# Evacuating projections from PSUM: both heads on ScalarE first, then both on VectorE, in a hybrid attention layer

## The chip, the cores and the metric

The kernel runs on one core of one Trainium2 chip. The metric is the device time of one execution in microseconds; the time before is the median of three runs, 699.13 us (698.71 to 699.32).

## The reference, cut to what matters

One encoder layer with 1024 positions of width 1024 in fp32. The input is normalised and modulated to `u`. One projection gives queries, keys, values and gates for 8 heads of forgetting attention (FoX) and 8 of stick-breaking attention, head width 64, and 8 forget-gate columns.

```python
h = u @ w_in[layer]
fq, fk, fv, fg, ff, sq, sk, sv, sg = _split_columns(h)
log_f = jax.nn.log_sigmoid(ff + b_f[layer])
f_cum = jnp.cumsum(log_f, axis=1).transpose(0, 2, 1)
...
# FoX, per block of 128 queries
s = einsum('bhqd,bhkd->bhqk', q, k) * scale + (f_q[..., :, None] - f_k[..., None, :])
p = softmax(where(causal, s, -inf));  out = p @ v
# stick-breaking
log_beta, log_keep = log_sigmoid(z), where(strict, log_sigmoid(-z), 0)
w = where(strict, exp(log_beta + cumsum_from_the_right(log_keep) - log_keep), 0);  out = w @ v
...
y = concatenate([y_fox * silu(fg), y_sb * silu(sg)]) @ w_out[layer]
x = layer_norm(alpha * x + gate * y)
```

## The kernel before, in words

**Tiling.** Heads go in eight pairs p, the two heads h of a pair on the lower and the upper 64 partitions. Pairs 0 to 3 are stick-breaking, 4 to 7 FoX. Queries go in eight blocks i of 128 positions. To keep fp32 precision every operand of TensorE is split into a high part, rounded to the matmul's format, and a low part, the remainder, and each product is made of three matmuls (hi x hi, hi x lo, lo x hi).

**Projections.** `gen_m(p, m)` makes the queries (m = 0), keys (1) or gates (2) of a pair in two chunks `ch` of 512 positions: 24 matmuls (L256 to L258) into one PSUM accumulator `m` of 64 + 64 partitions, then its evacuation. `evac_q` (L227) writes for each head the high part with ScalarE (L232) and the low part with VectorE (L233), `evac_k` (L236) likewise (L241, L244) and sends the high part to the other half of the partitions by a DMA on SyncE's queue (L243). `v_tile` (L305) makes 128 positions of the values of two pairs (L311 to L313) and evacuates them in two halves, one for each pair, with ScalarE (L319) and VectorE (L320); for one group it also takes the forget-gate columns (L323). There are two accumulators of this kind (`acc`), and TensorE can start a third chunk only when the first has been read in full.

**Attention.** `att_query` copies a query block to a padded tile `qz` (ScalarE, L389). `att_scores` makes the scores S (L411, L412) in a single PSUM buffer. In stick-breaking, ScalarE makes `kp` and `be` with two sigmoids (L430, L431), VectorE scans `kp` (L436, L440), and GpSimd multiplies it into `be` (L442, after a memset at L443). In FoX, VectorE adds the forget bias `fb` and takes the row's extreme (L418), adds the causal mask to the next block's part of `fb` (L396), ScalarE does the exponential (L423), VectorE a reciprocal (L424) and GpSimd the scaling (L425). `att_transpose` transposes the weights to a PSUM tile T (L459, two buffers) and splits it into `pt`: the high part by ScalarE (L461), the low part by VectorE (L462). `att_pv` multiplies them with the values (L474): first the products with the high part of `pt`, then those with the low part. Its sum is evacuated by ScalarE, VectorE and GpSimd in turn (L493 to L495).

**The forget logs** (`forget_logs`, L339) need Exp and Ln on ScalarE (L344, L345) between operations on VectorE (L343, L346, L349). Sigmoid, Exp and Ln lie in different function tables, and each change of table shows as an ACT_TABLE_LOAD.

**Weights** come in by DMA (`raw`) and are split by GpSimd into `whi` and `wlo` (L125, L126). GpSimd and VectorE also prepare the output gate early on (L698 to L701).

**What sets the order.** TensorE's order is written by hand: attention units and steps of the projections ("fillers") are interleaved by a table. During the start SyncE's is as well. The order of VectorE, ScalarE, GpSimd and the DMA queues in the main part is set by a scheduler that goes by a model of the engines' times; each engine then runs its instructions in that order. Where a wait by TensorE is short, those orders have placed the evacuations between attention operations.

Of the kernel before, what the change touches and what calls it, by code (L numbers as in the profile page):

```python
# [8 lines left out]
F32 = mybir.dt.float32  # L9
F32R = mybir.dt.float32r  # L10
AF = mybir.ActivationFunctionType
ALU = mybir.AluOpType

P = 128
# [4 lines left out]
HD = 64  # L19
EPS = 1e-5  # L20
ALPHA = 2.0 ** 0.25
SCALE = HD ** -0.5
# [5 lines left out]
def tile_hybrid_layer(  # L28
# [17 lines left out]
    nc = tc.nc  # L46
# [180 lines left out]
    def evac_q(p, ch, acc, qst, heads):  # L227
        s = slice(ch * 512, ch * 512 + 512)
        for h in heads:
            r = slice(h * HD, h * HD + HD)  # L230
            o = slice((1 - h) * HD, (1 - h) * HD + HD)
            nc.scalar.activation(qst[h][r, s], acc[r, :], AF.Copy, scale=SCALE)  # L232
            nc.vector.scalar_tensor_tensor(qst[h][o, s], acc[r, :], SCALE, qst[h].bitcast(F32)[r, s],  # L233
                                           op0=ALU.mult, op1=ALU.subtract)

    def evac_k(p, ch, acc, kst, klo, heads):  # L236
        s = slice(ch * 512, ch * 512 + 512)
        for h in heads:
            r = slice(h * HD, h * HD + HD)
            o = slice((1 - h) * HD, (1 - h) * HD + HD)  # L240
            first = nc.scalar.copy(kst[h][r, s], acc[r, :])  # L241
            kf = kst[h].bitcast(F32)
            nc.sync.dma_start(kf[o, s], kf[r, s])  # L243
            last = nc.vector.tensor_tensor(klo[r, s], acc[r, :], kf[r, s], op=ALU.subtract)  # L244
        return first, last

# [13 lines left out]
    qst, kst, klo, sgt, vt = {}, {}, {}, {}, {}  # L260
# [11 lines left out]
    def evac_m(p, m, ch, acc, heads=(0, 1)):  # L272
        if m == 0:
            evac_q(p, ch, acc, qst[p], heads)
        elif m == 1:
            return evac_k(p, ch, acc, kst[p], klo[p], heads)
        else:
            evac_g(p, ch, acc, sgt[p])
# [26 lines left out]
    def v_tile(g, t, acc, quarters):  # L305
        n = 264 if g == 1 else 256
        ts_ = slice(t * P, (t + 1) * P)
        for kt in range(NB):
            hi, lo = quarters[kt // 2]
            s = slice((kt % 2) * n, (kt % 2) * n + n)  # L310
            nc.tensor.matmul(acc[:, :n], u_hi[kt][:, ts_], hi[:, s], start=(kt == 0), stop=False)  # L311
            nc.tensor.matmul(acc[:, :n], u_lo[kt][:, ts_], hi[:, s], start=False, stop=False)  # L312
            nc.tensor.matmul(acc[:, :n], u_hi[kt][:, ts_], lo[:, s], start=False, stop=(kt == NB - 1))  # L313
            if kt == 3:
                yield
        for i in range(2):
            v4 = vt[2 * g + i].rearrange("p t (x c) -> p t x c", c=HD)
            a4 = acc[:, i * P:(i + 1) * P].rearrange("p (x c) -> p x c", c=HD)
            nc.scalar.copy(v4[:, t, 0::2, :], a4)  # L319
            nc.vector.tensor_tensor(v4[:, t, 1::2, :], a4, v4.bitcast(F32)[:, t, 0::2, :],  # L320
                                    op=ALU.subtract)
        if g == 1:
            nc.vector.tensor_tensor(fsb[:, :, t], acc[:, 256:264], bf_sb, op=ALU.add)  # L323
        yield

    def gen_v(g, quarters=None, tiles=range(NB)):
        n = 264 if g == 1 else 256
        if quarters is None:
            quarters = []
            for h in range(4):  # L330
                src = w_vf[h] if g == 1 else w_v[g - (g > 1), h]
                quarters.append(fetch_w(f"v{g}_{h}", src, 2 * n))
        yield
        if g:
            make_v(g)
        for t in tiles:
            yield from v_tile(g, t, acc_tile(f"v_{g}_{t}"), quarters)
# [387 lines left out]
    def v_first(t, acc):  # L725
        for _ in v_tile(0, t, acc, v0_w):
            pass
# [9 lines left out]
    for kb in range(NB):  # L737
# [5 lines left out]
        if kb < len(evacs):  # L743
            n, h = evacs[kb]
# [204 lines left out]
    for k in range(len(units) + LAG + 1):  # L949
        if k < len(units):  # L950
# [10 lines left out]
            p, h, i = units[k]  # L961
# [85 lines left out]
```

## Time and profile before

| | |
|---|---|
| median of three runs | 699.13 us |
| profiled execution | 699.99 us |
| its span, first to last instruction | 698.2 us |
| granted TensorE clock, mean | 0.996 |
| TensorE (PE) busy | 676.0 us, 4033 matmuls |
| VectorE (DVE) busy | 483.7 us |
| GpSimd (POOL) busy | 410.6 us |
| ScalarE (ACT) busy | 385.0 us |
| evacuation of a query chunk, per head | 0.59 us ScalarE (L232), 0.69 us VectorE (L233) |
| of a value tile, per pair | 0.27 us ScalarE (L319), 0.28 us VectorE (L320) |

The profile is of one execution; a row of the timeline has the start in us from the span's start, the duration in us, the engine, the line, the operation with its output and input, their shapes, the count, and in brackets how long the engine had been idle and what released it. A row of the waits has the waiting engine and line, the one waited for, the total in us, how many times, and the longest. A row grouped by line has its busy time and the mean of one in ns, then the idle time ahead of it with its releasers.

### The profile page before, as it was taken

To read this page: it belongs to the slowest core of one execution; us is meant where nothing else is said; L and a number is where in the kernel's file an instruction comes from. 1 tells how busy PE (TensorE), PEld (TensorE's weight loads), DVE (VectorE), ACT (ScalarE), POOL (GpSimd) and SP (SyncE) were. 2 spreads that over 40 slices of the span, in tenths; PEclk is the share of its full clock that TensorE was granted. 3 is DMA by queue.
4 is the path that set the end of the run, shared out by engine and by line. 5 is a ranking of instruction groups with operands and counts; after the bars stand their busy time and mean duration, and the time that the engine had idled before them with its cause. 6 is when DMAs were issued, how large, how long until landed. Compare 5 with 4: busy or idle time off the path is not lost.

```text
span 698.2 us, 11781 instructions
## 1 busy us (share of the span) xinstructions
PE 676.0 (97%) x4033; PEld 589.0 (84%) x4033; DVE 483.7 (69%) x931; ACT 385.0 (55%) x866; POOL 410.6 (59%) x530
## 2 busy tenths in 40 slices
PE   7999989999999999999999999999999999999995
PEld 4789887888997888889988877889988889888884
DVE  5985678767657676767686684758576767784644
ACT  5667567856658576666664554645564666531000
POOL 4560487656437566556388897868483464665412
PEclk9999999999999999999999999999999999999998
DMA  8953451112102122112144554345241299143301
GB/s 313 415 215 128 113 176 53 28 39 49 42 9 69 40 53 55 38 46 61 29 134 145 174 164 155 112 116 164 95 143 51 58 283 364 56 162 113 119 31 60
DMA packets 44027, 81.59 MB, mean 117 GB/s; under 512 B 5120, under 2 KB 18880, under 8 KB 43072
## 3 DMA queue, kind: packets, MB, share of 16 engines
q1 hardware_dynamic: 42816, 76.65, 33.5%
q10 hardware_dynamic: 1152, 4.19, 2.0%
q8 instruction: 32, 0.52, 0.3%
q14 instruction: 27, 0.22, 0.1%
HBM read 60.34 MB, written 16.29 MB: 110 GB/s over the span
## 4 chain that ended last, share of the span: by engine, by line
PE 76%; DVE 7%; DMA 5%; POOL 4%; ACT 4%; issue 3%; SPq 0%; POOLq 0%; DVEq 0%; ACTq 0%
PE pv L474 9%; PE m L256 8%; PE m L257 8%; PE m L258 8%; PE T L459 8%; PE o L835 4%; PE o L833 4%; PE o L834 4%; PE S L412 4%; PE S L411 4%; PE v L311 3%; PE v L313 3%; PE v L312 3%; DMA wss<-in_w_ss_dram 1%; DMA raw<-in_w_qkg_dram 1%
## 5 line engine op out<-in xcount | busy, mean ns | idle before, releaser
L256 PE MATMUL m<-uh,whi 128*128 128x512 f32 x304 | 126.3, 415 | 0.5 <-DVE kl L244 0.5
L257 PE MATMUL m<-ul,whi 128*128 128x512 f32 x304 | 119.8, 394 | 0.0
L258 PE MATMUL m<-uh,wlo 128*128 128x512 f32 x304 | 119.6, 394 | 0.0
L462 DVE TENSOR_TENSOR pt<-T,pt 128x512 fp32r<-128x512 f32 (+2 forms) x192 | 100.6, 550 | 16.1 <-ACT pt L461 14.9
L442 POOL TENSOR_TENSOR be<-be,kp 128x127 f32<-128x127 f32 (+3 forms) x64 | 77.1, 1205 | 34.9 <-DVE kp L440 25.9
L461 ACT CAST pt<-T 128x512 fp32r<-128x512 f32 (+2 forms) x192 | 85.7, 480 | 17.2 <-PE T L459 13.6
L436 DVE TENSOR_TENSOR_SCAN kp<-kp,floor 128x512 f32<-128x512 f32 (+2 forms) x64 | 65.2, 1018 | 32.4 <-ACT kp L430 31.4
L474 PE MATMUL pv<-pt,v 128*128 128x256 f32 (+3 forms) x640 | 81.7, 272 | 3.8 <-DVE pt L462 3.8
L474 PEld LDWEIGHTS pv<-pt,v 128*128 128x128 f32 (+1 forms) x640 | 77.4, 163 | 9.0 <-DVE pt L462 4.7
L425 POOL TENSOR_SCALAR a<-a,l 128x1024 f32<-128x1024 f32 (+3 forms) x64 | 48.3, 755 | 43.8 <-DVE l L424 31.2
L423 ACT ACTIVATE a<-a,nm 128x1024 f32<-128x1024 f32 (+3 forms) x64 | 49.8, 778 | 40.5 <-DVE nm L418 40.1
L258 PEld LDWEIGHTS m<-uh,wlo 128*128 128x128 f32 x304 | 57.1, 188 | 13.5
L411 PE MATMUL S<-k,q 128*128 128x512 f32 (+5 forms) x192 | 66.6, 348 | 1.5 <-ACT be L431 0.8
L412 PE MATMUL S<-kl,qz 128*128 128x512 f32 (+5 forms) x192 | 65.5, 342 | 0.0
L256 PEld LDWEIGHTS m<-uh,whi 128*128 128x128 f32 x304 | 57.3, 188 | 9.2 <-DVE kl L244 0.9
L257 PEld LDWEIGHTS m<-ul,whi 128*128 128x128 f32 x304 | 57.4, 189 | 8.0
L495 POOL TENSOR_TENSOR ty<-ty,sg 64x256 f32<-64x256 f32 x64 | 47.7, 745 | 26.5 <-DVE ty L494 12.5
L418 DVE CUSTOM_DVE_ANT_0 a<-S,fb 128x1024 f32<-128x1024 f32 (+3 forms) x64 | 48.2, 754 | 15.9 <-PE S L412 7.8
L430 ACT ACTIVATE kp<-S 128x128 f32<-128x128 f32 (+3 forms) x64 | 41.7, 651 | 31.9 <-PE S L412 28.6
L311 PE MATMUL v<-whi_v,uh 128*128 128x256 f32 (+1 forms) x192 | 56.0, 292 | 0.7 <-DVE kl L244 0.7
L389 ACT CAST qz<-q 64x128 fp32r<-64x128 f32 x128 | 37.4, 295 | 31.3 <-PE S L412 30.0
L313 PE MATMUL v<-wlo_v,uh 128*128 128x256 f32 (+1 forms) x192 | 54.2, 282 | 0.0
(284 smaller groups left out, 1628.6 us busy)
## 6 DMA issues: line engine op xcount, KB each, us to landing
raw<-in_w_qkg_dram SPq DMA_DIRECT2D x38, 256.0 KB, 3.0
wss<-in_w_ss_dram SPq DMA_DIRECT2D x7, 1024.0 KB, 9.0
x<-in_x_dram SPq DMA_DIRECT2D x8, 512.0 KB, 7.1
k<-k SPq DMA_DIRECT2D x32, 128.0 KB, 2.3
wg<-in_w_gate_dram SPq DMA_DIRECT2D x8, 512.0 KB, 5.0
raw_o<-in_w_out_dram SPq DMA_DIRECT2D x16, 256.0 KB, 2.7
fb<-f_dr ACTq DMA_DIRECT2D x8, 512.0 KB, 4.3
wo_dr<-whi_o SPq DMA_DIRECT2D x16, 256.0 KB, 2.4
```

The costliest lines, as they stand in the source:

```text
L256: nc.tensor.matmul(acc, hi[:, c], u_hi[kt][:, s], start=(kt == 0), stop=False)
L257: nc.tensor.matmul(acc, hi[:, c], u_lo[kt][:, s], start=False, stop=False)
L258: nc.tensor.matmul(acc, lo[:, c], u_hi[kt][:, s], start=False, stop=(kt == NB - 1))
L311: nc.tensor.matmul(acc[:, :n], u_hi[kt][:, ts_], hi[:, s], start=(kt == 0), stop=False)
L313: nc.tensor.matmul(acc[:, :n], u_hi[kt][:, ts_], lo[:, s], start=False, stop=(kt == NB - 1))
L411: nc.tensor.matmul(S[:, s, :w], qst[p][h][:, qs], kst[p][h][:, ks], start=True, stop=False)
L412: nc.tensor.matmul(S[:, s, :w], z, klo[p][:, ks], start=False, stop=True)
L436: nc.vector.tensor_tensor_scan(rv, rv, floor[0][:, 512 - n:][:, ::-1], initial=0.0, op0=ALU.mult, op1=ALU.max)
L442: nc.gpsimd.tensor_tensor(be[:, :ke - 1], be[:, :ke - 1], kp[:, 1:ke], op=ALU.mult)
L461: nc.scalar.copy(hi[:, :n, qo:qo + P], t3)
L462: nc.vector.tensor_tensor(lo[:, :n, qo:qo + P], t3, hi.bitcast(F32)[:, :n, qo:qo + P], op=ALU.subtract)
L474: nc.tensor.matmul(acc[:m, q0:256], vt[p][:, kb, h * P:h * P + m], pt[:, kb % 4, q0:], start=start, stop=stop)
```

## The change

Per accumulator there are two heads, or two pairs for values. Before, ScalarE and VectorE took turns: high part of head 0, low part of head 0, high part of head 1, low part of head 1. After, ScalarE writes both high parts, then VectorE both low parts. The same operations on the same data, in `evac_q`, `evac_k` and `v_tile`:

```diff
     def evac_q(p, ch, acc, qst, heads):
         for h in heads:
             r = slice(h * HD, h * HD + HD)
+            nc.scalar.activation(qst[h][r, s], acc[r, :], AF.Copy, scale=SCALE)
+        for h in heads:
+            r = slice(h * HD, h * HD + HD)
             o = slice((1 - h) * HD, (1 - h) * HD + HD)
-            nc.scalar.activation(qst[h][r, s], acc[r, :], AF.Copy, scale=SCALE)
             nc.vector.scalar_tensor_tensor(qst[h][o, s], acc[r, :], SCALE, qst[h].bitcast(F32)[r, s],
                                            op0=ALU.mult, op1=ALU.subtract)
...
     def evac_k(p, ch, acc, kst, klo, heads):
             first = nc.scalar.copy(kst[h][r, s], acc[r, :])
             kf = kst[h].bitcast(F32)
             nc.sync.dma_start(kf[o, s], kf[r, s])
+        for h in heads:
+            r = slice(h * HD, h * HD + HD)
+            kf = kst[h].bitcast(F32)
             last = nc.vector.tensor_tensor(klo[r, s], acc[r, :], kf[r, s], op=ALU.subtract)
...
     def v_tile(g, t, acc, quarters):
-        for i in range(2):
-            v4 = vt[2 * g + i].rearrange("p t (x c) -> p t x c", c=HD)
-            a4 = acc[:, i * P:(i + 1) * P].rearrange("p (x c) -> p x c", c=HD)
+        v4s = [vt[2 * g + i].rearrange("p t (x c) -> p t x c", c=HD) for i in range(2)]
+        a4s = [acc[:, i * P:(i + 1) * P].rearrange("p (x c) -> p x c", c=HD) for i in range(2)]
+        for v4, a4 in zip(v4s, a4s):
             nc.scalar.copy(v4[:, t, 0::2, :], a4)
+        for v4, a4 in zip(v4s, a4s):
             nc.vector.tensor_tensor(v4[:, t, 1::2, :], a4, v4.bitcast(F32)[:, t, 0::2, :],
                                     op=ALU.subtract)
```

The four reads of one accumulator stay in sequence. Before, each of them waits for the one ahead of it on the other engine. After, ScalarE's second follows its first without a wait, VectorE's first waits for both of ScalarE's, and VectorE's second waits for nothing more. TensorE's order is the same row by row; the scheduler's order on the other engines changes around the evacuations, and ScalarE has 812 instructions in place of 811.

VectorE at the evacuation of q_5, chunk 1 (near 394 us), before and then after. `q_0` and `q_1` are the two heads' halves, `m_0_1` the accumulator, `pt` the low part of transposed weights of pair 4, `a`, `nm` the FoX scores' evacuation (`S_1_7`: head 1, block 7), which is two rows:

```order
L233 SCALAR_TENSOR_TENSOR q_0_4446<-m_0_1_4559,q_0_4446 64x512
L462 TENSOR_TENSOR pt_4_0_1_0_4585<-T_0_2_0_4638,pt_4_0_1_0_4584 128x3x128
L418 ISA a_1_7_4661,nm_1_7_4662<-S_1_7_4656,fb_4121 128x1024
L418 ISA nm_1_7_4662 128x1
L233 SCALAR_TENSOR_TENSOR q_1_4447<-m_0_1_4559,q_1_4447 64x512
```

The same place on VectorE after the change:

```order
L235 SCALAR_TENSOR_TENSOR q_0_4446<-m_0_1_4559,q_0_4446 64x512
L235 SCALAR_TENSOR_TENSOR q_1_4447<-m_0_1_4559,q_1_4447 64x512
L424 ISA a_1_7_4661,nm_1_7_4662<-S_1_7_4656,fb_4121 128x1024
L424 ISA nm_1_7_4662 128x1
L468 TENSOR_TENSOR pt_4_0_1_0_4585<-T_0_2_0_4638,pt_4_0_1_0_4584 128x3x128
```

The second half moved up to the first, and `pt` moved behind the second half and behind the scores.

VectorE at the evacuation of k_6, chunk 1 (near 468 us), before and then after; `fb` is the causal mask's addition, `kl` the low part of the keys:

```order
L396 TENSOR_TENSOR fb_5482<-fb_5482,causal 128x128
L244 TENSOR_TENSOR kl_5316<-m_1_1_5421,k_0_5314 64x512
L462 TENSOR_TENSOR pt_5_0_1_0_5456<-T_0_2_0_5502,pt_5_0_1_0_5455 128x3x128
L418 ISA a_1_7_5537,nm_1_7_5538<-S_1_7_5532,fb_5047 128x1024
L418 ISA nm_1_7_5538 128x1
L244 TENSOR_TENSOR kl_5316<-m_1_1_5421,k_1_5315 64x512
```

The same place on VectorE after the change:

```order
L402 TENSOR_TENSOR fb_5482<-fb_5482,causal 128x128
L249 TENSOR_TENSOR kl_5316<-m_1_1_5421,k_0_5314 64x512
L249 TENSOR_TENSOR kl_5316<-m_1_1_5421,k_1_5315 64x512
L424 ISA a_1_7_5537,nm_1_7_5538<-S_1_7_5532,fb_5047 128x1024
L424 ISA nm_1_7_5538 128x1
L468 TENSOR_TENSOR pt_5_0_1_0_5456<-T_0_2_0_5502,pt_5_0_1_0_5455 128x3x128
```

Again `pt` went from the place behind the first half to the place behind the second half and the scores. In q_4 and k_4, chunk 1, `pt` moved behind the second half alone. In k_5 and q_6, chunk 1, the scores' L418 stands first, then the two halves, then `fb`, then the two rows of `pt`, which had stood ahead of `fb` and of the second half. In q_7, chunk 1, L418 and the two halves stand ahead of `pt`; in k_7, chunk 1, the two halves stand together ahead of the scores of the last block.

ScalarE around the forget logs (212 to 220 us), before and then after. `fab` is the log's working tile, `kp`, `be` the sigmoids of the stick-breaking pair 1 (head 1, block 7) and of the next pair:

```order
L430 ACTIVATE kp_1_7_2471<-S_1_7_2466 128x1024
L431 ACTIVATE be_1_7_2472<-S_1_7_2466 128x1024
L389 CAST qz_83<-q_1_1564 64x128
L344 ACT_TABLE_LOAD
L344 ACTIVATE fab<-fab 128x64
L345 ACT_TABLE_LOAD
L345 ACTIVATE fab<-fab 128x64
L461 CAST pt_1_1_2_0_2433<-T_1_5_0_2494 128x4x128
L461 CAST pt_1_1_2_1_2442<-T_1_5_1_2501 128x2x128
L430 ACT_TABLE_LOAD
```

The same place on ScalarE after the change:

```order
L350 ACT_TABLE_LOAD
L350 ACTIVATE fab<-fab 128x64
L436 ACT_TABLE_LOAD
L436 ACTIVATE kp_1_7_2471<-S_1_7_2466 128x1024
L437 ACTIVATE be_1_7_2472<-S_1_7_2466 128x1024
L395 CAST qz_83<-q_1_1564 64x128
L351 ACT_TABLE_LOAD
L351 ACTIVATE fab<-fab 128x64
L467 CAST pt_1_1_2_0_2433<-T_1_5_0_2494 128x4x128
L467 CAST pt_1_1_2_1_2442<-T_1_5_1_2501 128x2x128
L436 ACT_TABLE_LOAD
```

Exp moved ahead of `kp` and `be`, and one more table load stands between them.

## The prediction

> **What bounds the kernel now.** I read the head of the profile's page and its chain first.
>
> ```profile
> span 698.2 us, 11781 instructions
> PE 676.0 (97%) x4033; PEld 589.0 (84%) x4033; DVE 483.7 (69%) x931; ACT 385.0 (55%) x866; POOL 410.6 (59%) x530
> PE 76%; DVE 7%; DMA 5%; POOL 4%; ACT 4%; issue 3%; SPq 0%; POOLq 0%; DVEq 0%; ACTq 0%
> ```
>
> TensorE is busy for 97% of the span and carries 76% of the chain. VectorE, at 69%, and ScalarE, at 55%, matter only where TensorE has to wait for them, so the next view is the list of what TensorE waits for (in all, times, longest).
>
> ```profile
> PE pv L474 <- DVE pt L462: 3.8, 5, 1.6
> ...
> PE T L459 <- POOL be L443: 1.1, 1, 1.1
> ...
> PE S L411 <- ACT be L431: 0.8, 1, 0.8
> ...
> PE m L256 <- DVE kl L244: 0.5, 1, 0.5
> ```
>
> The largest wait, 3.8 us, is for pt, the low half of the transposed weights (L462), not for an evacuation. Evacuations reach TensorE directly for 0.5 us at L256. So there is little to win, and the question is what the new order does to the work that shares an in-order engine with the evacuations. The rows grouped by line give prices (busy in all, mean ns of one, then idle before).
>
> ```profile
> L320 DVE TENSOR_TENSOR v<-v,v 128x128 fp32r<-128x128 f32 x60 | 17.0, 284 | 9.3 <-ACT v L319 8.7
> L233 DVE SCALAR_TENSOR_TENSOR q<-m,q 64x512 fp32r<-64x512 f32 x24 | 16.5, 689 | 5.7 <-ACT q L232 5.1
> ```
>
> **What the change does to a pair.** No evacuation is added or removed; each pair stays two ScalarE operations (0.59 us) and two VectorE operations (0.69 us for both kinds), one after the other (the 0.59 stands in the rows of q_5 below), 2.56 us for a query or key chunk. Three hand-overs between engines become one. A hand-over costs almost nothing: in the group of rows around 395 us below, ScalarE's half ends at 393.62 and VectorE's starts at 393.65. Two fewer hand-overs are worth 0.06 us. What counts is that VectorE now starts one ScalarE operation later (some 0.5 to 0.59 us), then runs 1.38 us in one piece, and that whatever stood between the halves stands elsewhere. A value pair is small (0.28 us an operation on VectorE), and TensorE's waits name no value evacuation, so I count the value tiles at nothing: the matmuls of the next tile cover them; bare, each would cost or win up to 0.28 us.
>
> **q_5, chunk 1, near 394 us: +1.5 us.** Rows of ScalarE, VectorE and TensorE:
>
> ```profile
> 393.03 0.59 ACT L232 ACTIVATE q<-m 64x512 fp32r<-64x512 f32 x1 [1.55 <-PE m L258]
> 393.65 0.68 DVE L233 SCALAR_TENSOR_TENSOR q<-m,q 64x512 fp32r<-64x512 f32 x1 [0.27 <-ACT q L232]
> 394.37 0.56 DVE L462 TENSOR_TENSOR pt<-T,pt 128x384 fp32r<-128x384 f32 x1
> 394.84 1.22 DVE L418 CUSTOM_DVE_ANT_0 a<-S,fb 128x1024 f32<-128x1024 f32 x1
> 395.49 1.00 PE L474 MATMUL pv<-pt,v 128*128 128x256 f32 x8
> ```
>
> Today pt is done at 394.93. Afterwards both ScalarE halves end at about 394.2 (393.03 + 2 x 0.59), then 0.68 and 0.69 for the VectorE halves (395.55), 1.22 for L418 (396.8), 0.56 for pt: 397.35. TensorE's eight products start at 395.49 on the high half of pt; at 0.12 us each the three of them last until 395.85, where the low half is needed. 397.35 - 395.85 = 1.5 us of waiting. Bounds: 1.0, if L418 can't start ahead and pt slips in faster than its row, and 2.0, if a hold-up like that of L396 (below) falls in.
>
> **k_6, chunk 1, near 468 us: +1.9 us.** VectorE and TensorE:
>
> ```profile
> 467.80 0.67 DVE L244 TENSOR_TENSOR kl<-m,k 64x512 fp32r<-64x512 f32 x1
> 468.40 0.54 DVE L462 TENSOR_TENSOR pt<-T,pt 128x384 fp32r<-128x384 f32 x1
> 468.87 1.20 DVE L418 CUSTOM_DVE_ANT_0 a<-S,fb 128x1024 f32<-128x1024 f32 x1
> 469.00 0.74 PE L474 MATMUL pv<-pt,v 128*64 128x256 f32 x5 [0.15 <-DVE pt L462]
> ```
>
> Here TensorE already waits 0.15 us for pt, so there is no slack. The first half starts when it does today, since both of ScalarE's operations are done before; then pt moves behind the second half (0.69) and L418 (1.20): 1.89 us later, all of it on the path. Bounds 1.2 (only L418) and 2.4.
>
> **Four like places: +2.6 us.** In q_4 chunk 1 (304 us), k_4 chunk 1 (320), k_5 chunk 1 (414) and q_6 chunk 1 (450) pt also goes behind the second half. The first of them:
>
> ```profile
> 303.57 0.42 DVE L462 TENSOR_TENSOR pt<-T,pt 128x256 fp32r<-128x256 f32 x1
> 304.22 0.58 PE L474 MATMUL pv<-pt,v 128*128 128x256 f32 x4
> ```
>
> pt starts 0.69 us later for the second half and up to 0.5 more because the first now waits for ScalarE's second operation: 303.57 + 1.2 + 0.42 = 305.2. Two of the four products use the high half, so the low one is needed at 304.5: 0.7 us. Each place lies between 0 (pt hidden) and 1.2 (both delays bare); I take 0.65 for each of the four. In the other chunks that the change reorders, pt has over 2 us until its product, or is not moved: nothing.
>
> **The forget logs, 212 to 221 us: +2.5 us.** ScalarE, VectorE, GpSimd, TensorE:
>
> ```profile
> 212.26 1.03 ACT L430 ACTIVATE kp<-S 128x1024 f32<-128x1024 f32 x1
> ...
> 214.54 1.28 ACT L344 ACT_TABLE_LOAD   x1
> 215.83 0.26 ACT L344 ACTIVATE fab<-fab 128x64 f32<-128x64 f32 x1
> ```
>
> ```profile
> 213.44 0.87 DVE L343 SCALAR_TENSOR_TENSOR fab<-fsb 128x64 f32<-128x64 f32 x1
> 214.23 1.21 DVE L436 TENSOR_TENSOR_SCAN kp<-kp,floor 128x512 f32<-128x512 f32 x1
> 215.48 1.28 DVE L440 TENSOR_TENSOR_SCAN kp<-kp,floor 128x512 f32<-128x512 f32 x1
> 217.69 1.23 DVE L346 SCALAR_TENSOR_TENSOR flf<-fsb,fab 128x64 f32<-128x64 f32 x1 [0.94 <-ACT fab L345]
> 218.95 1.26 DVE L349 TENSOR_TENSOR_SCAN fsb<-flf,later 128x64 f32<-128x64 f32 x1
> ```
>
> ```profile
> 216.84 2.00 POOL L442 TENSOR_TENSOR be<-be,kp 128x1023 f32<-128x1023 f32 x1 [0.47 <-DVE kp L440]
> 218.79 2.51 POOL L126 TENSOR_TENSOR wlo<-raw,whi 128x512 fp32r<-128x512 f32 x2
> ```
>
> ```profile
> 220.85 0.98 PE L474 MATMUL pv<-pt,v 128*64 128x256 f32 x7 [1.64 <-DVE pt L462]
> ```
>
> Because the value tile before it is evacuated differently, the scheduler puts Exp (L344) ahead of the last kp and be of the second head, and so needs one more table load on ScalarE. Exp cannot start before L343 ends at 214.31. From there: 0.26 for Exp, 1.28 for the load, two sigmoids of 1.03 (217.9; qz after them fits in their overlap), the load for Ln 1.28, Ln 0.26: 219.5, where L346 starts at 217.69 today. Kp is ready at 216.9, its two scans (1.21 and 1.28) end at 219.4, and GpSimd's 2.00 us product runs to about 221.4. That matters: L346 and L349 have 64 elements a lane, yet took 1.23 and 1.26 us, and ended within 0.1 us of a GpSimd operation's end (218.84; the first of the two at 218.79, about 220.05). Held in the same way, L346 ends at 221.45, L349 near 222.7, and TensorE resumes 0.64 us after its end, as today (220.85 against 220.21): 223.35. Without the hold-up, at 0.28 us each (the L320 row), VectorE would be free at about 220.1, as today, and TensorE lose some 0.4 us to ScalarE's later high part. So +0.4 to +2.9; I take 2.5, since both rows are held today. The Trainium skill, "SBUF — State Buffer", section "Who interferes with whom", has a VectorE instruction with two SBUF inputs blocked for the whole of a GpSimd instruction that reads SBUF; this trace agrees (1.23 us for 64 elements), and by that rule the upper part of the span is the right one.
>
> On the load itself the rows say 1.28 us, with Exp 0.01 us behind it. The Trainium skill, "ScalarE: Activation LUTs", section "What ACT_TABLE_LOAD costs", adds a drain of about 1.38 us to each switch; by it the sum would be 1.4 us higher, and this trace does not show it.
>
> **What is won: -0.7 us at 90 to 99 us, and -0.5 at 562.**
>
> ```profile
> 90.59 0.59 ACT L232 ACTIVATE q<-st_q1b 64x512 fp32r<-64x512 f32 x1 [1.40 <-DVE q L233]
> ...
> 94.67 0.58 ACT L241 CAST k<-st_k1b 64x512 fp32r<-64x512 f32 x1 [1.32 <-DVE kl L244]
> ```
>
> ```profile
> 92.06 1.31 POOL L699 TENSOR_TENSOR gate<-gate,wg 128x512 f32<-128x512 f32 x1 [1.06 <-ACT wg L698]
> ```
>
> ScalarE's second key half waited 1.32 us for VectorE, and be, behind it on ScalarE, held TensorE for 0.8 us (the S row of TensorE's waits). That wait goes. Next late is GpSimd's be, for which TensorE's first transpose waits 1.1 us; it moves forward only as far as GpSimd's gate sums do, whose 1.06 us of waiting for ScalarE shrinks too, as ScalarE no longer waits 1.40 us at 90.59. Between 0 (GpSimd unmoved) and -0.8 (all of it); I take -0.7. At 562 the second half of k_7 stood behind L418 and held an accumulator: the 0.5 us of the L256 row of TensorE's waits goes.
>
> **Sum.** 1.5 + 1.9 + 2.6 + 2.5 - 0.7 - 0.5 = +7.3 us on the profiled execution's 699.99 (span 698.2 and 1.8 around it), 707.3. That execution lies 0.86 above the median of 699.13, so I forecast 706.4.
>
> **Rivals.** *Faster.* Accumulators come free as a pair, TensorE's next chunk starts earlier, and pt is fast enough everywhere: it holds if TensorE's products have more queued ahead of the low half than I count. For it speak TensorE's waits that the halves in turn cause now: 0.8 for be, 0.5 at L256 and about half of the 1.1 for GpSimd's be, -1.9 us in all: 697.2. It decides at 468 us: there the low half is needed the moment it is ready, which speaks against it. Chance 0.09. *No change*: only 468 us hurts (+1.9), and the two gains (-1.2) nearly pay for it: 699.8; chance 0.08. *Half of it*: GpSimd does not hold L346, and the four like places are half hidden: 1.5 + 1.9 + 0.6 + 0.3 - 1.2 = +3.1, 702.2; chance 0.20. *Worse*: at k_5 and q_6, L396 now stands ahead of pt, and one such operation was held for a long time:
>
> ```profile
> 404.77 4.15 DVE L396 TENSOR_TENSOR fb<-fb,causal 128x128 f32<-128x128 f32 x1
> ```
>
> If one or both meet a busy GpSimd, pt comes some 1.3 us later at each (one L126, 2.51 for two): about +3, 709.4; chance 0.13. The forecast keeps 0.50.
>
> **Chances and range.** The measurement can tell about 0.2%, 1.4 us. Faster 0.09, same 0.08, slower 0.83, which are the cases above. The range reaches from below the half case, 701.0, to the worse case, 709.8; the first two rivals, 0.17, lie outside.
>
> **What would show it.** Right: TensorE's waits for pt grow from 3.8 us to about 10, with single waits near 1.5 to 2 us at q_5 and k_6 chunk 1; one more table load, and L346 over 1 us long; no wait for be near 95 us. Wrong: products at q_5 and k_6 that start without a wait for pt, or a forget stretch that is not longer than today's 8.6 us (212.26 to 220.85).

## The result, and the profile after

The changed kernel takes 708.24 us, median of 4 runs (708.14 to 709.12), against 699.12 (698.71 to 699.32): 1.0133 times as long, interval 1.012 to 1.0147, or 9.1 us more. The forecast was 706.4, the range 701.0 to 709.8.

The profiled execution took 708.33. The head of its page, then the list of what TensorE waits for (in all, times, longest):

```profile
span 706.6 us, 11831 instructions
PE 680.3 (96%) x4033; PEld 592.7 (84%) x4033; DVE 481.7 (68%) x931; ACT 386.4 (55%) x867; POOL 411.0 (58%) x530
```

```profile
PE pv L480 <- DVE pt L468: 11.0, 9, 2.6
...
PE S L417 <- ACT be L437: 0.8, 2, 0.5
PE pv L480 <- ACT pt L467: 0.5, 1, 0.5
```

The wait for pt grew from 3.8 to 11.0 us. TensorE's busy time grew too, from 676.0 to 680.3 us, with the same 4033 matmuls, so part of the loss is no wait: the matmuls themselves took longer somewhere. The rows in which the evacuations held TensorE (v and m, both waiting for kl) are gone.

TensorE's order is the same in both kernels, so each matmul's start can be set against its start before. Where that difference jumps, time went or came. Up to 540 us:

| place (time before) | jump, us | running total |
|---|---|---|
| 96 us, first be | -0.94 | -0.8 |
| 99 us, GpSimd's be | -1.24 | -2.2 |
| 180 us, k_2 | -0.90 | -3.1 |
| 215 to 221 us, forget logs: four waits | +0.33, +0.66, +0.65, +0.96 | -0.35 |
| 221 to 224 us: no wait, slower matmuls | +1.6 | +1.25 |
| 269 us, k_3 | +0.5 | +1.8 |
| q_4, k_4 | +0.96, +0.74 | +3.6 |
| q_5 | +1.66 | +5.2 |
| 410 us; k_5 | -0.85; +0.85 | +5.1 |
| 434 us, the mask's L396 | -1.28 | +3.8 |
| q_6 | +1.64 | +5.4 |
| k_6 | +1.98 | +7.4 |
| 469 to 472 us: no wait, slower matmuls | +1.55 | +9.0 |

At q_7 -0.66 and +0.62 cancel, k_7 gives -0.53, and it ends at +8.4, the difference of the spans. The -0.85 and the -1.28 are not the change's: a kernel below that keeps the turns from 200 us on (early_only) shows the same jumps there, -0.85 and -1.31. They are delays that before's profiled execution had; how many of before's other executions had them is not known.

The forget stretch after, on ScalarE, VectorE, GpSimd and TensorE (start, duration; in brackets the wait ahead of it):

```profile
211.18 0.26 ACT L350 ACTIVATE fab<-fab 128x64 f32<-128x64 f32 x1 [0.90 <-DVE fab L349]
211.45 1.28 ACT L436 ACT_TABLE_LOAD   x1
...
215.02 1.28 ACT L351 ACT_TABLE_LOAD   x1
216.32 0.26 ACT L351 ACTIVATE fab<-fab 128x64 f32<-128x64 f32 x1
```

```profile
216.61 1.97 DVE L352 SCALAR_TENSOR_TENSOR flf<-fsb,fab 128x64 f32<-128x64 f32 x1 [0.19 <-ACT fab L351]
218.61 1.25 DVE L355 TENSOR_TENSOR_SCAN fsb<-flf,later 128x64 f32<-128x64 f32 x1
219.79 0.99 DVE L468 TENSOR_TENSOR pt<-T,pt 128x512 fp32r<-128x512 f32 x2
```

```profile
216.50 2.00 POOL L448 TENSOR_TENSOR be<-be,kp 128x1023 f32<-128x1023 f32 x1 [1.02 <-DVE kp L446]
218.45 2.50 POOL L126 TENSOR_TENSOR wlo<-raw,whi 128x512 fp32r<-128x512 f32 x2
```

```profile
220.50 1.34 PE L480 MATMUL pv<-pt,v 128*64 128x256 f32 x7 [2.59 <-DVE pt L468]
```

L352 is done as GpSimd's product is (218.58 and 218.50), L355 as the first of the two L126 is (about 219.7). Add 3.16, the lead that the changed kernel had there, and these are the forecast's instants plus about 0.3 us: L346's end 221.74 (221.45), L349's 223.02 (222.7), TensorE 223.66 (223.35). The 0.3 us is the query copy qz (0.29 us), which stands between be and the load for Ln; the forecast had let it vanish in an overlap. ScalarE has one instruction more, 867 for 866: the added load.

k_6, chunk 1, on VectorE and TensorE, and the windows around TensorE's restart (length, busy time of PE, PEld, DVE, ACT and POOL, then the granted clock, DMA share, GB/s):

```profile
473.28 1.38 DVE L249 TENSOR_TENSOR kl<-m,k 64x512 fp32r<-64x512 f32 x2
474.69 1.23 DVE L424 CUSTOM_DVE_ANT_0 a<-S,fb 128x1024 f32<-128x1024 f32 x1
475.84 0.08 DVE L424 DVE_READ_ACCUMULATOR2_ANT nm<- 128x1 f32 x1
475.84 0.55 DVE L468 TENSOR_TENSOR pt<-T,pt 128x384 fp32r<-128x384 f32 x1
```

```profile
473.86 0.46 PE L480 MATMUL pv<-pt,v 128*128 128x256 f32 x3
476.45 0.88 PE L480 MATMUL pv<-pt,v 128*64 128x256 f32 x5 [2.13 <-DVE pt L468]
```

```profile
474.50:476.30 1.80, 0.00 (x0) 0.00 (x0) 1.77 (x4) 0.34 (x1) 0.74 (x2) 1.00 0.85 261
476.50:477.50 1.00, 1.00 (x8) 1.00 (x8) 0.25 (x2) 0.80 (x3) 1.00 (x1) 0.70 0.79 301
477.50:478.50 1.00, 1.00 (x7) 1.00 (x6) 0.67 (x2) 0.65 (x2) 1.00 (x2) 0.50 0.02 6
...
480.50:481.50 1.00, 1.00 (x8) 0.95 (x7) 0.66 (x3) 0.56 (x3) 0.90 (x3) 1.00 0.03 10
```

pt stands behind 1.38 and 1.23 us of other work, TensorE waits 2.13 us, and then the granted clock falls to 0.50 for 3.4 us (the record has it from 476.91 to 480.32). PE is "busy" all through: only the clock column and the count of matmuls show the loss. The same fall follows the wait of 2.59 us at the forget logs.

### The profile page after: what moved, and what is told of

Its sections match the earlier page's. It is cut to its first block, busy times and chain, and to the rows that moved or that the text cites. A ratio compares the mean times of both kernels' runs of the same rounds, so it can differ in the third digit from the quotient of the medians.

```text
span 706.6 us, 11831 instructions
## 1 busy us (share of the span) xinstructions
PE 680.3 (96%) x4033; PEld 592.7 (84%) x4033; DVE 481.7 (68%) x931; ACT 386.4 (55%) x867; POOL 411.0 (58%) x530
## 4 chain that ended last, share of the span: by engine, by line
PE 49%; DVE 2%; POOL 1%; issue 1%; DMA 1%; ACT 0%; POOLq 0%; DVEq 0%
PE pv L480 6%; PE T L465 5%; PE m L261 5%; PE m L262 5%; PE m L263 5%; PE o L839 4%; PE o L841 4%; PE o L840 4%; PE S L418 3%; PE S L417 3%; PE v L316 2%; PE v L318 2%; PE v L317 2%; DVE a L424 1%; DMA fb<-f_dr 1%
## 5 line engine op out<-in xcount | busy, mean ns | idle before, releaser
L480 PE MATMUL pv<-pt,v 128*128 128x256 f32 (+3 forms) x640 | 83.2, 274 | 11.5 <-DVE pt L468 11.0
L418 PE MATMUL S<-kl,qz 128*128 128x512 f32 (+5 forms) x192 | 65.5, 342 | 0.0
L499 ACT COPY ty<-pv 64x256 f32<-64x256 f32 x64 | 23.5, 367 | 60.0 <-PE pv L480 41.5
```

The lines of the kernel that those rows point to most:

```text
L418: nc.tensor.matmul(S[:, s, :w], z, klo[p][:, ks], start=False, stop=True)
L480: nc.tensor.matmul(acc[:m, q0:256], vt[p][:, kb, h * P:h * P + m], pt[:, kb % 4, q0:], start=start, stop=stop)
```

## The experiments

My theory: the loss is pt queued behind the pairs on VectorE, plus the moved Exp with GpSimd's hold of VectorE, with a slowed TensorE behind long waits; the early places gain. The rivals: the loss is in the evacuations themselves, or the whole comes from one of the three functions. Each ratio is to the kernel before on the same chip; there it took 699.12 us for the first four, 699.49 for exp_behind, pool_behind, no_idle and both_mended, 698.71 for the rest.

**One function at a time.** In q_only, k_only and v_only one of `evac_q`, `evac_k` and `v_tile` is as after, the others as before. For q_only:

```diff
         for h in heads:
             r = slice(h * HD, h * HD + HD)
-            o = slice((1 - h) * HD, (1 - h) * HD + HD)
             nc.scalar.activation(qst[h][r, s], acc[r, :], AF.Copy, scale=SCALE)
+        for h in heads:
+            r = slice(h * HD, h * HD + HD)
+            o = slice((1 - h) * HD, (1 - h) * HD + HD)
             nc.vector.scalar_tensor_tensor(qst[h][o, s], acc[r, :], SCALE, qst[h].bitcast(F32)[r, s],
```

> The kernel before, with only the queries' evacuation in the new order (the order of ScalarE and VectorE around the forget logs is then that of the kernel before). Main theory (what costs is pt, moved behind the second half and the scores on VectorE, place by place): +1.0 at q_4 chunk 1, +1.7 at q_5, +1.6 at q_6, 0 at q_7, less up to 1.3 us where a later TensorE finds the fb transfer near 433 us done: +2.5 to +4.3 us, 701.6 to 703.4. Rival (the later start of VectorE, which waits for both ScalarE halves, costs at every chunk alike): a third of the whole +9, 702.1, but spread over all 16 query chunks of the trace. Rival (the forget logs and table load are all of it): 699.1.

Measured: 701.17 us (699.79 to 703.06), 1.0035 [1.0022, 1.0048]. q_4, q_5 and q_6 lose 0.95, 1.66 and 1.36 us, against 0.96, 1.66 and 1.64 in after. The query chunks between 102 and 303 us lose nothing: the difference to before stays within 0.05 us there, so VectorE's later start does not cost at every chunk alike. One loss of 2.37 us was not foreseen and is not in after: here the scheduler put GpSimd's next weights ahead of its be, and they wait for their transfer.

```profile
101.53 0.62 POOL L125 TENSOR_SCALAR whi<-raw 128x512 fp32r<-128x512 f32 x1 [3.17 <-DMA raw<-in_w_qkg_dram]
```

For k_only:

```diff
             nc.sync.dma_start(kf[o, s], kf[r, s])
+        for h in heads:
+            r = slice(h * HD, h * HD + HD)
+            kf = kst[h].bitcast(F32)
             last = nc.vector.tensor_tensor(klo[r, s], acc[r, :], kf[r, s], op=ALU.subtract)
```

> The kernel before, with only the keys' evacuation in the new order. Main theory: -0.9 near 95 us, -0.9 near 180 us, +0.6 at k_3, +0.7 at k_4, about 0 at k_5, +2.0 and 1.5 of a slowed TensorE at k_6, -0.5 at k_7: +2.5 us, 701.6. Rival (VectorE's later start at every chunk alike): 702.1, spread over all chunks. Rival (forget logs alone): 699.1.

Measured: 701.42 us (699.5 to 702.77), 1.0031 [1.002, 1.0043]. It has -0.94 at 96 us, -0.90 at 180, +0.47 at k_3, +0.75 at k_4 and +1.98 at k_6; k_5 cost +0.45 and +0.73, where nothing was expected. The wait of 2.13 us at k_6 was followed by no slow stretch in this execution.

For v_only:

```diff
-        for i in range(2):
...
+        for v4, a4 in zip(v4s, a4s):
             nc.scalar.copy(v4[:, t, 0::2, :], a4)
+        for v4, a4 in zip(v4s, a4s):
             nc.vector.tensor_tensor(v4[:, t, 1::2, :], a4, v4.bitcast(F32)[:, t, 0::2, :],
```

> The kernel before, with only the values' evacuation in the new order. It moves Exp ahead of kp and be near 212 us, with one more table load, as the whole change does. Main theory: all of the forget stretch and nothing else, +4.4 us, less up to 1.3 at the fb transfer near 433 us: 702.2 to 703.5. Rival (values cost or win at each tile): a difference spread over the 30 tiles at 100 to 130, 175 to 215, 330 to 375 and 470 to 510 us.

Measured: 703.33 us (700.1 to 704.82), 1.0055 [1.0039, 1.0071]. The value pairs alone move Exp and bring the table load; the forget logs cost 0.33, 0.65, 0.63 and 0.96 us of waits, and behind 100 us nothing else moved by as much as 0.5 us but TensorE's wait for the mask at 434 us (-1.14, as above). From 100 to 214 us, across the values' tiles, the difference to before begins and ends within 0.02 us, so the tiles themselves cost nothing there. The profiled execution was the shortest of the ten, and in it TensorE's clock stayed at 1.00 behind the wait. Each function has its own places at which it loses, so no single one explains the change.

**pt_first: VectorE's halves behind pt.** At seven places where pt was overtaken, the VectorE pair is held back and issued behind pt (the expectation counts them as six; q_7 is left as in after). ScalarE's and TensorE's orders stay those of after; GpSimd's changes here and there, mostly from 410 to 432 and from 474 to 497 us.

```diff
+            soon(nc.vector.scalar_tensor_tensor, qst[h][o, s], acc[r, :], SCALE, qst[h].bitcast(F32)[r, s],
+                 op0=ALU.mult, op1=ALU.subtract)
...
             att_transpose(u)
+            for n, (f, a, kw) in enumerate(held):
+                with after(*([pt_lo[0]] if True else [])):
+                    f(*a, **kw)
```

> The kernel after, in which at six places (q_3 or q_4 chunk 0, and chunk 1 of q_4, k_4, q_5, k_5, q_6, k_6) both VectorE halves are put behind pt; each pair stays a pair, ScalarE's order is untouched. Main theory: the waits for pt of 1.0, 0.7, 1.7, 0.9, 1.6 and 2.0 us go or shrink to 0.7 at k_6, and so does the slowed TensorE there (1.5); the gain near 433 us is given back: 701 (700 to 702.5). Rival (pairs cost because VectorE starts later and holds accumulators): pairs end later still, so 708.2 or more.

Measured: 700.43 us (700.16 to 701.8), 1.0024 [1.0013, 1.0035], 7.8 us below the changed kernel. The waits for pt fall from nine to four:

```profile
PE pv L488 <- DVE pt L476: 4.0, 4, 2.6
```

The 2.6 is the forget logs'; at q_5 0.25 and at k_6 0.55 us stay, and at k_5 TensorE now waits 0.42 us for ScalarE's half of pt. The other held places are clear. The pairs themselves are still there: their place in VectorE's queue was the cost.

**exp_behind: Exp back behind kp and be.** The forget logs are issued two rows later, Exp behind the second head's be.

```diff
+        with after(last_be[0]):
+            nc.scalar.activation(ab, ab, AF.Exp, scale=-1.0)
...
     def gen_forget():
+        for _ in range(FLATE):
+            yield
         logs = forget_logs()
-        for _ in range(FROW):
+        for _ in range(FROW - FLATE):
             yield
```

> The kernel after, with Exp of the forget logs behind kp and be of pair 1, head 1, block 7, as in the kernel before, by starting the logs two steps later; one table load fewer. Main theory: the forget stretch is as before the change, -4.4 us: 703.8 (703 to 705). Rival (only the extra table load of 1.28 us counts): 707.

Measured: 705.58 us (703.36 to 706.83), 1.0087 [1.0071, 1.0103]. Of the engines' orders only ScalarE's differs from after. The added table load is gone, and with it three of the four jumps (the first, +0.34, stays) and the slow stretch at 221 us: from 180 to 230 us the kernel now gains 0.4 us where after loses 4.4. The time lies above the 703 to 705 expected, but on the same chip a repeat of the changed kernel, next, took 710.35: 4.8 us more, for 4.4 expected. One of the logs' two VectorE operations is still held, beside GpSimd's product (215.21 to 217.21 us):

```profile
215.14 0.23 DVE L356 SCALAR_TENSOR_TENSOR flf<-fsb,fab 128x64 f32<-128x64 f32 x1
215.40 1.97 DVE L359 TENSOR_TENSOR_SCAN fsb<-flf,later 128x64 f32<-128x64 f32 x1
```

So GpSimd's hold alone is not the loss.

**pool_behind: GpSimd's product ordered behind the logs.** The order was given only as a preference.

```diff
+            with after(*logs_done if u == (1, 1, 7) else ()):
+                nc.gpsimd.tensor_tensor(be[:, :ke - 1], be[:, :ke - 1], kp[:, 1:ke], op=ALU.mult)
```

> The kernel after, with every engine's order as it is; GpSimd's product of pair 1, head 1, block 7 (be x kp, 2.00 us) only waits until the forget logs' two small VectorE operations are done. Main theory (those two, 1.97 and 1.25 us in the profile after, are held by GpSimd's operations): the first takes about 0.3 us, the wait of 2.6 us for pt at the forget logs shrinks to about 0.5, and the stretch of slowed TensorE behind it (1.4 us) goes: 704 to 706. Rival (operations of 64 elements take that long by themselves): they keep 1.2 to 2 us, and the product comes later: 708.2 or more.

Measured: 710.35 us (709.11 to 711.82), 1.0158 [1.0142, 1.0175]. The expectation missed because the edit did nothing: no engine's order changed, and since nothing on GpSimd waits for VectorE's logs, the product started at 216.88, ahead of L354 at 217.00. So this is the changed kernel again, L354 1.96 and L357 1.26 us long.

**pool_waits: the same with a dependence.** VectorE rewrites one column of kp behind the logs, times one; GpSimd's product reads it and has to wait.

```diff
+            if u == (1, 1, 7):
+                with after(*logs_done):
+                    nc.vector.tensor_scalar(kp[:, 1:2], kp[:, 1:2], 1.0, 1.0, op0=ALU.mult, op1=ALU.mult)
             nc.gpsimd.tensor_tensor(be[:, :ke - 1], be[:, :ke - 1], kp[:, 1:ke], op=ALU.mult)
```

> The kernel after; pair 1, head 1, block 7's product on GpSimd now really waits for the forget logs, through a one-column copy on VectorE issued behind them (the column times 1.0, so its value stays). If GpSimd's operations hold the two small VectorE operations: the first takes about 0.3 us in place of 1.97, the second under 0.5 in place of 1.25, TensorE's wait of 2.6 us for pt shrinks below 0.6 and no slowed stretch follows: 4 us under the kernel after (6 to 7 us over the kernel before on the same chip). If small operations take that long of themselves: unchanged or slower than the kernel after.

Measured: 704.91 us (704.82 to 706.62), 1.0095 [1.0082, 1.0109]. VectorE's logs, GpSimd's product and TensorE:

```profile
216.82 0.23 DVE L354 SCALAR_TENSOR_TENSOR flf<-fsb,fab 128x64 f32<-128x64 f32 x1 [0.20 <-ACT fab L353]
217.08 0.29 DVE L357 TENSOR_TENSOR_SCAN fsb<-flf,later 128x64 f32<-128x64 f32 x1
```

```profile
217.50 2.00 POOL L453 TENSOR_TENSOR be<-be,kp 128x1023 f32<-128x1023 f32 x1 [1.82 <-DVE kp L452]
```

```profile
217.31 1.74 PE L485 MATMUL pv<-pt,v 128*128 128x256 f32 x12 [0.48 <-ACT pt L472]
```

The same two operations take 0.23 and 0.29 us where GpSimd stands still, against 1.97 and 1.25 beside its product and its L126. The wait of 2.59 us is gone, and from 180 to 230 us the kernel loses 0.1 us in place of 4.4, with the added table load still in it (211.66 us). The moved Exp and its load are not free, though: the jumps of 0.33, 0.65 and 0.65 us ahead of that wait stay. They are paid for because before had a wait of 1.64 us of its own behind the same two operations (1.23 and 1.26 us there), and that is gone as well (-1.68). So the loss takes both, logs that come late and GpSimd's hold, and either cure undoes it; what each costs alone, no run separates.

**no_idle: TensorE kept busy at k_6.** Eighteen transposes into an unused tile fill the wait.

```diff
         product(0, last)
+        if (p, h, j) == (5, 0, 1):
+            spin = t_tile("spin")
+            for _ in range(18):
+                nc.tensor.transpose(spin[:, :P], ident, ident)
```

> The kernel after, with 18 transposes of the identity matrix (about 1.9 us, into a spare PSUM tile, their result unused) between the high and the low products of pair 5, head 0, second block pair, where TensorE waits 2.1 us for pt at k_6 and then ran at a granted clock of 0.50 for some 3 us. If the slow stretch comes from TensorE having been idle: it goes, -1.5 us, 706.7. If it comes from anything else at that place (the DMA traffic, the matmuls after it): 708.2, slow stretch as before. If the transposes themselves cost: above 708.2.

Measured: 709.46 us (709.08 to 709.69), 1.0143 [1.0128, 1.0158], 0.9 below the repeat of after on that chip, whose interval it meets. In the profile the filling works, and the clock behind it is 1.00:

```profile
476.92 2.15 PE L491 MATMUL spin<-ident 128*128 128x128 f32 x18
```

```profile
479.40:480.40 1.00, 1.00 (x11) 1.00 (x11) 0.16 (x1) 0.92 (x3) 1.00 (x1) 1.00 0.83 309
```

Behind the spare transposes the kernel loses nothing more, where after loses 1.55. But at k_5 this execution had a wait of 2.33 us, 1.07 us more than after's, and at the forget logs its clock stayed at 0.50 for 6.83 us in place of 3.41 (2.7 us lost for 1.6), so by its total it decides nothing.

**both_mended: pt_first and the preference of pool_behind together.**

```diff
+                with after(*([pt_lo[0]] if True else [])):
...
+            with after(*logs_done if u == (1, 1, 7) else ()):
```

> The kernel after with both mends: VectorE halves behind pt at the six places (pt_first, 700.4), and GpSimd's product behind the forget logs (pool_behind). Main theory: what the new order wins near 95 us (2.1), 180 us (0.9) and 562 us (0.6) is left over, and the forget stretch is no longer than before: 700.4 less 2 to 3 us, 697.5 to 698.4, faster than the kernel before by 0.7 to 1.6. Rival (the pairs cost in ways that the places don't show): 699.5 or more.

Measured: 701.6 us (699.98 to 702.34), 1.0032 [1.0021, 1.0043]. A miss for the same reason as pool_behind: the second edit did nothing, and this repeats pt_first.

**early_only: the pairs only where they gain.** The kernel before, with pairs for queries up to pair 1 and keys up to pair 2.

```diff
+    def evac_q(p, ch, acc, qst, heads):
+        if p > 1:
+            return evac_q_turns(p, ch, acc, qst, heads)
...
+        if p > 2:
+            return evac_k_turns(p, ch, acc, kst, klo, heads)
```

> The kernel before, with pairs only in the evacuations of the start (pairs 0 and 1) and the keys of pair 2; from 200 us on every engine's order is that of the kernel before. Main theory: the waits of 0.9 and 1.2 us near 95 and 99 us and of 0.9 near 180 us go, nothing else moves: -2 to -3 us against the kernel before on the same chip. Rival (these gains are given back at the next wait for a transfer): within 0.5 us of it.

Measured: 696.45 us (694.92 to 696.68), 0.9964 [0.9953, 0.9975]. The places give -0.94, -0.81 and -0.90.

**pt_and_exp: the changed kernel with both cures,** pt_first's edit and exp_behind's:

```diff
+                with after(*([pt_lo[0]] if True else [])):
...
+        with after(last_be[0]):
+            nc.scalar.activation(ab, ab, AF.Exp, scale=-1.0)
```

> The kernel after, with VectorE's halves behind pt at the six places (as in pt_first) and with Exp behind kp and be at the forget logs (as in exp_behind). Main theory: both costs gone, the early gains left over: 2 to 3 us under the kernel before on the same chip, and no stretch of slowed TensorE, since no wait over 2 us is left. Rival (pairs cost beside these places): equal to it or above.

Measured: 695.68 us (695.08 to 696.18), 0.9957 [0.9945, 0.997]: 3.0 us less than before, and below the changed kernel too. The waits for pt:

```profile
PE pv L492 <- DVE pt L480: 2.4, 4, 1.0
```

No wait behind 90 us is over 2 us and no slow stretch is left. What remains is the gain of the early places, -2.7 in this execution (-0.94, -0.84, -0.90), and about what early_only has. That both cures together take the whole loss away shows that the loss was those two things and what follows from them.

**v_only_again: v_only once more,** with no edit against it, for the spread of its ten runs.

> v_only once more, for a second profile: its ten runs lay between 700.1 and 704.8 us, and the one profiled was the fastest. If TensorE's slowed stretch behind the forget logs' wait of 2.6 us comes in some runs and not in others, this run shows it or not, worth 1.1 to 1.4 us; if the values' tiles cost by themselves, the difference lies at them.

Measured: 702.39 us, one run. One window behind the wait at the forget logs, in v_only and then in the repeat (the column after POOL is the clock):

```profile
223.60:224.60 1.00, 1.00 (x9) 1.00 (x10) 1.00 (x3) 0.00 (x0) 0.80 (x3) 1.00 0.59 201
```

```profile
223.40:224.40 1.00, 0.97 (x5) 0.97 (x6) 1.00 (x3) 0.00 (x0) 0.80 (x3) 0.50 0.72 156
```

Five matmuls in place of nine: the same program has the slow stretch in one execution and not in the other. It is worth 1.4 us of the 2.3 between the two; 0.76 is a wait for the mask's fb at 434 us. Whether these two make up the whole spread of v_only, 4.7 us, stays open.

## Why the prediction was right, point by point

**q_5 and k_6, the two places with quoted orders: right in mechanism and size.** Forecast 1.5 and 1.9, measured 1.66 and 1.98. At q_5 the new row of VectorE is the sum's own: 1.39 for the pair, 1.23, 0.55 for pt.

```profile
397.81 1.39 DVE L235 SCALAR_TENSOR_TENSOR q<-m,q 64x512 fp32r<-64x512 f32 x2 [0.92 <-PE S L418]
399.23 1.23 DVE L424 CUSTOM_DVE_ANT_0 a<-S,fb 128x1024 f32<-128x1024 f32 x1
...
400.38 0.55 DVE L468 TENSOR_TENSOR pt<-T,pt 128x384 fp32r<-128x384 f32 x1
```

pt_first shows the cause: behind pt, the same pairs cost 0.25 and 0.55 us there. But the k_6 term had no place for what TensorE does after the wait, +1.55.

**Four like places: too small.** Forecast 2.6, measured 0.96 + 0.74 + 0.85 + 1.64 = 4.2. The step that failed is the middle value of 0.65 for each; q_6 went past its bound of 1.2, since the mask's L402 stands ahead of pt there as well:

```profile
453.81 1.39 DVE L235 SCALAR_TENSOR_TENSOR q<-m,q 64x512 fp32r<-64x512 f32 x2
455.23 0.58 DVE L402 TENSOR_TENSOR fb<-fb,causal 128x128 f32<-128x128 f32 x1
455.84 1.16 DVE L468 TENSOR_TENSOR pt<-T,pt 128x512 fp32r<-128x512 f32 x2
```

The rival "worse" had named L396, at 1.3 us more if held; it took 0.58.

**The forget logs: right in mechanism, too small.** Forecast +2.5; TensorE resumed 2.8 us later than before, relative to the lead it had, and lost 1.6 more to the halved clock: 4.4. Of the 2.8 only 0.96 is the last wait's growth; the rest fell on three waits ahead of it, which the forecast had not told apart. The hold-up by GpSimd, argued from two rows (which ended 0.08 and 0.16 us behind GpSimd's, not both within 0.1), is shown by pool_waits: 1.97 and 1.25 us become 0.23 and 0.29. That the forecast's low end, +0.4 without the hold-up, is real shows there too, at +0.1. Ln starts 0.02 us behind its table load (215.02 + 1.28 = 216.30, 216.32). The drain of 1.38 us that the Trainium skill, "ScalarE: Activation LUTs", section "What ACT_TABLE_LOAD costs", adds to each switch is again not in the trace.

**The early gain: too small.** Forecast -0.7 at 90 to 99 us, with a bound of -0.8; measured -0.94 and -1.24. The failed step is the bound: it held that once the 0.8 us for ScalarE's be is gone, GpSimd's be is late in its place. But GpSimd's be came 2.2 us earlier (98.73 to 96.54), so TensorE's wait of 1.1 us for it went as well. The forecast had counted only the gate sums' second wait for ScalarE, 1.06 us; their first shrank by 1.7, as the rows of before and after show:

```profile
87.99 3.02 POOL L699 TENSOR_TENSOR gate<-gate,wg 128x512 f32<-128x512 f32 x2 [2.62 <-ACT wg L698]
```

```profile
86.42 3.00 POOL L705 TENSOR_TENSOR gate<-gate,wg 128x512 f32<-128x512 f32 x2 [0.91 <-ACT wg L704]
```

At 180 us the forecast had nothing, and -0.90 came, by the mechanism that it used at 562. The rows of before, first from TensorE's waits, then from VectorE's timeline:

```profile
PE v L311 <- DVE kl L244: 0.7, 1, 0.7
```

```profile
177.71 1.28 DVE L440 TENSOR_TENSOR_SCAN kp<-kp,floor 128x512 f32<-128x512 f32 x1
179.02 0.69 DVE L244 TENSOR_TENSOR kl<-m,k 64x512 fp32r<-64x512 f32 x1
```

The second half of k_2 stood behind two scans and held the value tile's accumulator. After, both halves start at 173.42. That row stood in the list of TensorE's waits, and the forecast left it out when it put what TensorE waits directly for evacuations at 0.5 us. k_7's -0.5 was right (-0.53). The +0.5 at k_3, where TensorE now waits for ScalarE's be, was not foreseen.

**The sum.** Forecast +7.3 in the profiled execution, measured +8.4. By places, measured less forecast: pt +1.8 (q_5, k_6 and the like places, 7.8 for 6.0), k_3 +0.5, the forget logs' waits +0.3, the two slow stretches +3.2, the early places -2.4, and -2.1 that belongs to before's execution; together +1.3, the +1.1 but for rounding and small jumps. The total came out near because misses of both signs nearly cancel, which is luck; the two largest, the slow stretches and the early gain, were each as large as a term. By the medians, +9.1, the sum is 1.8 short. The "half of it" rival was also added up too low: half of 2.6 is 1.3 where it takes 0.6, and the low end of the forget logs is 0.4 where it takes 0.3, which makes 703.0 and not 702.2. What stands by experiment is the direction and its two causes.

## What to carry to other kernels

Before engine operations are paired on an in-order queue, ask which operation with a waiting consumer they overtake: its delay is the sum of the durations put ahead of it, and here that forecast two places to 0.2 us. Look at what GpSimd does at that instant before pricing a small VectorE operation by its size: here the same one took 0.23 or 1.97 us. Go through every row of the bounding engine's waits, since each one that names the moved operations is a gain or a loss of its own; here the best kernel kept the gains and gave pt its place back.

## What was not expected of the hardware

**Half the clock behind a wait of about two microseconds.** In the stretches after 90 us of the kernels here, TensorE's waits of 2.1 to 2.6 us went with a granted clock of 0.50 in 10 cases of 14. In 8 of them it lasted 3.41 us and cost 1.4 to 1.6 us; in 2 (no_idle and both_mended, at the forget logs) it lasted 6.83 us and cost 2.7 and 2.8. In 4 the clock stayed at 1.00, after waits of 2.13, 2.20, 2.33 and 2.60 us. Behind waits of up to 1.86 us it never fell. The fall begins anywhere from 0.9 us before TensorE resumes to 1.5 us after, so it is not the wait's end that sets it.

The Trainium skill, "TensorE: Matmul & The Clock Gate", section "Part 1: The HAM clock gate", puts the state of half clock after at least one idle window of about 3.4 us, and says that the window runs free of the kernel. Here 2.1 us were enough, so the figure does not hold as a threshold for a wait; the free-running window does fit. In each trace every change of the clock lies a whole number of 3.413 us behind the first record: in after, whose first stands at 9.28 us, the changes at 220.91, 224.32, 476.91 and 480.32 us are 62, 63, 137 and 138 of these steps on. With each trace cut into these steps, the step ahead of each of the 10 falls held 1.93 to 2.62 us of TensorE's idle time, and in all 14 traces no step at full clock that was followed by another held more than 1.76. In the two long cases the first step at half clock held another 0.91 and 0.78 us; where it held 0.45 or less, the clock was back after one. So one and the same program can go either way. In v_only an edge at 222.15 cuts the wait of 2.60 us, and neither step is idle enough (busy for 1.79 and 1.96 of 3.41 us); in the repeat most of it falls into one step (busy for 0.80), and the next runs at half clock:

```profile
218.74:222.15 3.41, 1.79 (x10) 1.12 (x8) 3.18 (x3) 3.37 (x8) 2.55 (x2) 1.00 0.00 0
222.15:225.56 3.41, 1.96 (x16) 1.92 (x17) 3.06 (x6) 1.57 (x6) 2.34 (x4) 1.00 0.36 99
```

```profile
219.56:222.97 3.41, 0.80 (x5) 0.65 (x5) 3.38 (x3) 3.09 (x7) 3.41 (x3) 1.00 0.00 0
222.98:226.39 3.41, 2.96 (x15) 2.96 (x16) 2.06 (x5) 0.79 (x2) 1.60 (x4) 0.50 0.59 154
```

no_idle, where the wait at k_6 was filled, had clock 1.00 there, which agrees; it is one execution. Where between 1.76 and 1.93 us the limit lies, no run here shows.

**A preference in the order is no wait.** Two runs asked GpSimd's product to stand behind VectorE's logs; across engines that changed nothing until the product read what VectorE wrote.
